# A decoder block on one core: scores of both attention maps on half the rows each, whole q and k loads, and four smaller moves

## The chip, the cores and the metric

The kernel runs on one core of one Trainium2 chip. The metric is the device time of one execution in microseconds, lower is better. The kernel is compared with a changed version of itself on the same inputs. The engines are named as in the profile: PE is TensorE's matmul, PEld its weight load, DVE is VectorE, ACT is ScalarE, POOL is GpSimd and SP is SyncE, which here issues most of the transfers.

## What is computed

One layer of a decoder with sequence 1024, width 1024 and float32 data. A norm of x feeds one input projection and sigmoid gates; three mixers work on the projection; the gated sum goes through an output projection; then comes a gated feed-forward part (FFN) with a causal convolution, and a final norm. The part that matters here is the third mixer: causal differential attention with four heads, each with two maps of 64 dimensions and one value of 128, and a position bias shared by both maps.

```python
def diff_attn_mixer(zq, zk, zv, lam_vecs, subln_g, rel_bias, layer_idx):
    ...
    s = jnp.einsum('bqhcd,bkhcd->bhcqk', qi, k) * scale      # c: the two maps
    s = s + bias.transpose(2, 0, 1)[None, :, None]
    s = jnp.where((rel >= 0)[None, None, None], s, -1e30)
    p = jax.nn.softmax(s, axis=-1)
    a = p[:, :, 0] - lam * p[:, :, 1]
    ...
    return rmsnorm(out, subln_g, eps=1e-5) * (1.0 - lam_init)

def reference(x, ...):
    h = rmsnorm(x, attn_norm_g); z = h @ w_in
    gates = sigmoid(h @ w_gate + b_gate)
    merged = g_a * (y_a @ proj_a) + g_b * (y_b @ proj_b) + g_c * (y_c @ proj_c)
    x = x + merged @ w_out
    x = x + conv_ffn(rmsnorm(x, ffn_norm_g), w_up, conv_w, conv_b, w_down)
    return rmsnorm(x, final_norm_g)
```

## The kernel before

Activations are kept transposed: 128 features on the rows, sequence positions on the columns, 512 columns to a PSUM bank. A float32 operand is split into a rounded high part and a low part (`split`, lines 96 and 97: a cast on ACT, a subtraction on DVE), and each product is three matmuls, high by high, high by low and low by high (`mm3`, line 191, with the list `PASSES`). The big products are done by a seven-product Strassen scheme, `strassen_pair` for pairs of output blocks and `strassen_full` for the output projection and the last FFN product. `strassen_pair` calls a hook `mid` four times, so that other work can be put between its products.

The order of the work is: norm and first mixers to 130 us; the q, k and pooling projections to 196 us; twelve gate pairs to 437 us, whose results go to DRAM (`g_d`); attention to 592 us, with the merge of the first two mixers (`merge_ab`, the "filler") between; the merge of the third (`merge_c`) to about 655 us; the output projection to about 725 us; the FFN to 1157 us; and its last product to the end. The instructions of an engine run in the order in which a scheduler set them when the kernel was built; a wait on one therefore holds back those behind it.

Attention works on tiles of 128 queries, `tiles` (head, i); a tile has (i + 1) x 128 keys, in one or two chunks of at most 512. `scores(t, c)` handles one map c of tile t: for each chunk two matmuls on 128 rows, with the stationary operand `qs` that holds the high part of q on rows 0 to 63 and its low part on 64 to 127, and the moving operands `kh` and `kl`, which hold the high (low) part of k on both halves of the rows (lines 759 and 760). DVE adds the bias tile T and takes the running minimum (line 762), ACT takes the exponential (line 768). `combine` subtracts the maps on DVE, `transpose` turns the tile on PE (tag "at"), `attend` multiplies it with the values V (tag "ms"). The PSUM banks are: three for scores ("sc"), two "at", one "ms", two "mm" for the merge and the norm of the heads.

`load_head` brings a head's operands from DRAM. Each map's `qs`, `kh` and `kl` are filled by two transfers of 64 rows each (line 716), 12 for a head; then come T from the bias table `fsc` and V, gathered from `v_d` in pieces of 128 columns. `rel_bias` makes the bias table after the first q and k pair: three matmuls with 33 rows and 4 columns (line 390), a copy on ACT, a store to `frow`, and four broadcasts from `frow` to `fsc`, all issued by SP.

Tiles come from two pools, `w4` of 13 tiles (weights, and other short-lived ones) and `a4` of 34. The output projection is `strassen_full` with four weight blocks; its passes p run in the order 0, 1, 2, 3, 5, 4, and loads are issued four items ahead (`loads`; `wfull` is line 843, `wh` line 835), in SP's order.

After the output projection `rms_mid` computes the FFN norm's factor for each half through `rms4a` and `rsqrt`: a square root on ACT, a reciprocal and one Newton step on DVE. `done1` prepares the operands T1 to T4 of the FFN's first products; they are made while the first FFN pair runs.

Of the kernel before, what the change touches and what calls it, by code (L numbers as in the profile page):

```python
# [11 lines left out]
F32 = mybir.dt.float32  # L12
I32 = mybir.dt.int32
F32R = mybir.dt.float32r
AF = mybir.ActivationFunctionType
# [3 lines left out]
P = 128  # L19
# [3 lines left out]
NH = 512  # L23
DFF = 2816
FT = DFF // P
NHEAD = 4
# [21 lines left out]
def trunk_kernel(  # L48
# [19 lines left out]
    nc = tc.nc  # L68
# [14 lines left out]
    def a4(shape=None, dt=F32, n="a"):  # L83
        return ap_.tile(shape or [P, S], dt, tag="a", name=nm(n))

    def w4(shape=None, dt=F32, n="w"):
        return wp.tile(shape or [P, S], dt, tag="w", name=nm(n))
# [4 lines left out]
    def tiny(n, tag, bufs=4):  # L92
        return sm.tile([P, n], F32, tag=tag, name=nm(tag), bufs=bufs)
# [57 lines left out]

        rms4b(rms4a(sq, pool), hs, pool)

    def rms4a(sq, pool):
        ps = pool()
        ss_cols(ps, sq, 4, 1, 0)
        t = tiny(4, "ssum")
        nc.vector.tensor_scalar(out=t, in0=ps[:, :4], scalar1=1.0 / D, scalar2=1e-6, op0=ALU.mult, op1=ALU.add)
        return rsqrt(t, 4)

    def rms4b(r, hs, pool):
        bcast_rows(r, 4, RB[:, hs], pool)
# [220 lines left out]
    def rel_bias():  # L383

        for c0 in range(0, NREL, NH):
            n = min(NH, NREL - c0)
            oh, fb = c2("oh"), c2("fb")
            nc.sync.dma_start(out=oh[:33, :n], in_=oneh[:, c0:c0 + n])
            pf = pm1()
            nc.tensor.matmul(pf[:NHEAD, :n], lhsT=rb, rhs=oh[:33, :n], start=True, stop=True)  # L390
            nc.scalar.mul(fb[:NHEAD, :n], pf[:NHEAD, :n], -1.0)
            nc.sync.dma_start(out=frow[:, c0:c0 + n], in_=fb[:NHEAD, :n])
        for hd in range(NHEAD):
            nc.sync.dma_start(out=fsc[hd], in_=frow[hd:hd + 1, :].broadcast_to([P, NREL]))

# [96 lines left out]


    qk_d = dram.tile([8, 2, P, S], F32, name="qk_d")
    v_d = dram.tile([8, P, NH], F32, name="v_d")
    y_d = dram.tile([4, P, S], F32, name="y_d")
    g_d = dram.tile([24, P, S], F32, name="g_d")
    x1_d = dram.tile([KT, P, S], F32, name="x1_d")
# [3 lines left out]
    def values():  # L502
# [32 lines left out]
        def store(o, banks, c, r, i):  # L535

            for b in range(2):
                TT(out=o[b], in0=banks[b], in1=c[b], op=ALU.add)
                for t in range(2):
                    sl = o[b][:, t * 256:(t + 1) * 256]  # L540
                    nc.scalar.mul(sl, sl, R8[:, 4 * i + 2 * b + t:4 * i + 2 * b + t + 1])
                tt = 4 * i + 2 * b
                nc.sync.dma_start(out=v_d[tt:tt + 2, :, r * 256:(r + 1) * 256].rearrange("t p c -> p t c"),
                                  in_=o[b].rearrange("p (t c) -> p t c", t=2))

        def wide(n):
            t = w4([P, 2, NH], n=n)
# [123 lines left out]
    for z in zb:  # L671
        times_r(z, nc.vector)

    rel_bias()


    def store_qk(i, Fs, eng=None):
        for n_, F in enumerate(Fs):
# [27 lines left out]

    def load_head(hd):

        H = heads[hd] = dict(qkl=[])
        for c in range(2):  # L710
            q, kh, kl = (a4(dt=F32R, n=n) for n in ("qs", "kh", "kl"))
            r = slice(64 * c, 64 * c + 64)
            for dst, src in ((q[0:64], qk_d[hd, 0, r]), (q[64:128], qk_d[hd, 1, r]),
                             (kh[0:64], qk_d[4 + hd, 0, r]), (kh[64:128], qk_d[4 + hd, 0, r]),
                             (kl[0:64], qk_d[4 + hd, 1, r]), (kl[64:128], qk_d[4 + hd, 1, r])):
                nc.sync.dma_start(out=dst.bitcast(F32), in_=src)
            H["qkl"].append((q, kh, kl))
            if c == 0:
                H["T"] = a4(n="T")
                base = fsc[hd]  # L720
                skew = bass.AP(tensor=base.tensor, offset=base.offset + P - 1, ap=[[NREL - 1, P], [1, S]])
                nc.sync.dma_start(out=H["T"], in_=skew)
            yield
        H["V"] = a4([P, 8, P], n="V")
        nc.sync.dma_start(out=H["V"], in_=v_d[:, :, hd * P:(hd + 1) * P].rearrange("t p c -> p t c"))
        yield
        H["s0"], H["ss"] = tiny(8, "s0", 2), tiny(8, "so", 2)
        H["O"] = a4([P, 8, P], n="O")
# [7 lines left out]
    st, AH = {}, {}  # L736
    score_bank = [pm1]

    def scores(t, c):

        if t >= len(tiles):
            return
        hd, i = tiles[t]
        H = heads[hd]
        W = (i + 1) * P
        if c == 0:
            if W <= NH:
                b = a4([P, 2, NH], n="sc")
                st[t] = dict(pr=[b[:, 0, :], b[:, 1, :]], s=[])
            else:  # L750
                st[t] = dict(pr=[a4(n="sc"), a4(n="sc")], s=[])
        q, kh, kl = H["qkl"][c]
        sc_ = st[t]["pr"][c]
        mx = tiny(2, "mx")
        chunks = [(0, min(NH, W))] + ([(NH, W - NH)] if W > NH else [])
        for n_, (c0, n) in enumerate(chunks):
            ps = score_bank[0]()
            qs = q[:, i * P:(i + 1) * P]
            nc.tensor.matmul(ps[:, :n], lhsT=qs, rhs=kh[:, c0:c0 + n], start=True, stop=False)  # L759
            nc.tensor.matmul(ps[:, :n], lhsT=qs, rhs=kl[:, c0:c0 + n], start=False, stop=True)  # L760
            o = (7 - i) * P + c0
            nc.vector.tensor_tensor_reduce(  # L762
                out=sc_[:, c0:c0 + n], in0=ps[:, :n], in1=H["T"][:, o:o + n], scale=1.0,
                scalar=mx[:, 0:1] if n_ else 3.0e38,
                op0=ALU.add, op1=ALU.min, accum_out=mx[:, n_:n_ + 1])
        nm_ = mx[:, n_:n_ + 1]
        sum_ = H["s0"][:, i:i + 1] if c == 0 else tiny(1, "s1")
        nc.scalar.activation(out=sc_[:, :W], in_=sc_[:, :W], func=AF.Exp, bias=nm_, scale=-1.0, accum_out=sum_)
        st[t]["s"].append(sum_)

    for n_ in range(12):
        Fs = strassen_pair(w_gate[n_], h, pb1)
        for k, F in enumerate(Fs):
            m = 2 * n_ + k
            times_r(F)
            nc.scalar.activation(out=F, in_=F, func=AF.Sigmoid, bias=col(C_BG + m), scale=1.0)
            nc.sync.dma_start(out=g_d[m], in_=F)
# [31 lines left out]
    def strassen_full(src, w, nsl, x_d, out, done, tail=None, LL=4):  # L809
# [29 lines left out]

        def wfull(p, j):  # L840
            if (p, j) not in halves:
                t = w4(n="fr")
                nc.sync.dma_start(out=t, in_=w[j])
                halves[p, j] = t
            return halves[p, j]
# [154 lines left out]

    ngain = const.tile([P, KT], F32, name="ngain")
    nc.scalar.mul(ngain, cs[:, C_GF:C_GF + KT], -1.0)
    tprep = [], []

    def op_g(src, g, n):

# [6 lines left out]
    def done1(d, j):  # L1013
# [45 lines left out]
            tprep[0].extend((t1, t2, t3))  # L1059
            return [store, operand, square]  # L1060
        if (d // 4, j) == (1, 0):
            tprep[1].append(t4)
            return [store, operand, square]
        return [store, square, operand]

# [8 lines left out]
            return p2.tile([P, NH], F32, tag=tag, name=nm(tag), bufs=bufs)  # L1074
        return f

    score_bank[0], pat, pms, pmm = pt2("sc", 3), pt2("at", 2), pt2("ms", 1), pt2("mm", 2)

    def combine(t):

# [126 lines left out]

    wo = strassen_full(lambda k: mg[k], w_out, 4, xT, lambda d, j: x1[d][:, half(j)], done1)
    LL = 4
    mc = merge_c([pmm, pmm, *score_bank * 3, pat, pat])  # L1210
    lates = []
    for t in range(len(tiles) + 3):
        hd, i = tiles[min(t, 31)]
# [71 lines left out]
            nc.scalar.copy(F0[k][:, half(j)], ps[k])  # L1285

    def rms_mid():
        for j in (1, 0):
            rs[j] = rms4a(stat[j], pb3)
            yield  # L1290
            rms4b(rs[j], half(j), pb3)
            yield
        stat.clear()
# [243 lines left out]
```

## Time and profile before

| what | value |
|---|---|
| time, median of 3 runs | 1388.32 us (1386.16 to 1389.51) |
| the profiled execution, its own time | 1389.13 us |
| its span, first to last instruction | 1387.4 us |
| mean granted TensorE clock | 0.991 |
| PE / PEld busy | 1344.9 us (97%) / 1120.5 us (81%) |
| DVE / ACT / POOL busy | 964.5 (70%) / 652.4 (47%) / 495.9 us (36%) |
| data moved by DMA | 204.65 MB, mean 148 GB/s |

A row of the timeline has start, duration, engine, line, operation, output and inputs, their shapes, how many instructions it joins, and, in brackets, how long the engine was idle before it and what ended that. The end of a matmul is modelled, so the cost of one is read from start to start. A busy share is an average over a stretch; an engine can be busy and still not be what the next one waits for.

### The profile page before, as it was taken

The numbers are of one execution on the slowest core, as the hardware profiler recorded it, in microseconds if no ns is written. First come the engines' busy times: TensorE is split into PE (matmuls) and PEld (weight loads), VectorE is DVE, ScalarE is ACT, GpSimd is POOL, SyncE is SP. The second block draws the span as 40 slices with busy tenths as digits, with TensorE's granted clock in tenths as the row PEclk, the third lists the DMA queues.
The fourth block names the chain that finished last, engine by engine and source line by source line (L and its number), as shares of the span: only waits on it lengthen the run. The fifth ranks groups of instructions, "written<-read, shape, count | busy, mean of one in ns | idle before, by whom it ended". The sixth has DMA issues, their size and how long they took to land.

```text
span 1387.4 us, 17666 instructions
## 1 busy us (share of the span) xinstructions
PE 1344.9 (97%) x6454; PEld 1120.5 (81%) x6454; DVE 964.5 (70%) x1487; ACT 652.4 (47%) x1109; POOL 495.9 (36%) x327
## 2 busy tenths in 40 slices
PE   9999999999999989999999999999999999999997
PEld 7997778888887778877777888888888887878786
DVE  7985774445444879958769576666777669985853
ACT  8633343344433666723667343433343435455461
POOL 0022334455553000022221665666656640102014
PEclk9999999999999999999999999999999999999998
DMA  7023363333239898588795222212222248845853
GB/s 261 10 78 109 108 222 134 121 121 104 101 115 272 252 242 209 151 233 193 201 221 131 83 77 91 79 74 91 91 77 91 75 151 305 274 126 150 226 128 122
DMA packets 78831, 204.65 MB, mean 148 GB/s; under 512 B 8270, under 2 KB 17614, under 8 KB 78744
## 3 DMA queue, kind: packets, MB, share of 16 engines
q1 hardware_dynamic: 67224, 180.44, 39.4%
q0 software_dynamic: 11520, 23.07, 9.7%
q8 instruction: 51, 0.84, 0.2%
q14 instruction: 36, 0.29, 0.1%
HBM read 143.70 MB, written 47.46 MB: 138 GB/s over the span
## 4 chain that ended last, share of the span: by engine, by line
PE 67%; DVE 13%; DMA 10%; issue 6%; ACT 3%; POOL 1%; SPq 1%; DVEq 0%; POOLq 0%; ACTq 0%
PE b L191 59%; PE mm L191 2%; DMA fr<-in_w_down 2%; DMA pr<-in_w_proj 1%; DVE ft L97 1%; PE ms L1112 1%; DVE fw L97 1%; DMA qs<-qk_d 1%; POOL ga L104 1%; DMA fr<-in_w_out 1%; DVE sc L762 1%; DMA x<-in_xT 1%; DMA yr<-y_d 1%; PE sc L759 1%; ACT fw L96 1%
## 5 line engine op out<-in xcount | busy, mean ns | idle before, releaser
L191 PE MATMUL b<-ft,fw 128*128 128x512 f32 (+1 forms) x1308 | 293.0, 384 | 9.8 <-ACT x L912 3.4
L191 PEld LDWEIGHTS b<-ft,fw 128*128 128x128 f32 x1308 | 239.9, 189 | 60.3 <-DVE fw L97 4.0
L354 POOL TENSOR_TENSOR F<-F,RB 128x1024 f32<-128x1024 f32 x68 | 185.5, 2730 | 111.3 <-DVE F L262 110.2
L262 DVE TENSOR_TENSOR F<-b,c 128x512 f32<-128x512 f32 x152 | 100.9, 683 | 130.5 <-ACT c L281 58.3
L191 PE MATMUL b<-hb,Ah 128*128 128x512 f32 x608 | 190.2, 392 | 0.0
L191 PE MATMUL b<-T,Sh 128*128 128x512 f32 x504 | 155.8, 390 | 1.9 <-ACT c L272 1.9
L234 POOL TENSOR_TENSOR s<-r 128x512 f32<-128x512 f32 x36 | 54.4, 1512 | 224.3 <-DMA r<-in_w_up 84.2
L191 PEld LDWEIGHTS b<-hb,Ah 128*128 128x128 f32 x608 | 114.5, 189 | 24.0 <-issue 0.5
L191 PE MATMUL b<-hb,Al 128*128 128x512 f32 x304 | 119.5, 393 | 2.5 <-DVE Al L97 2.5
L97 DVE TENSOR_TENSOR Al<-r,Ah 128x1024 fp32r<-128x1024 f32 x38 | 56.1, 1476 | 94.0 <-issue 77.9
L97 DVE TENSOR_TENSOR Sl<-s,Sh 128x1024 fp32r<-128x1024 f32 x76 | 107.0, 1408 | 13.9 <-ACT Sh L96 8.5
L96 ACT CAST Sh<-s 128x1024 fp32r<-128x1024 f32 x76 | 80.0, 1052 | 75.6 <-PE b L191 43.2
L191 PEld LDWEIGHTS b<-T,Sh 128*128 128x128 f32 x504 | 94.6, 188 | 21.8 <-ACT c L272 2.4
L191 PE MATMUL b<-T,Sl 128*128 128x512 f32 x252 | 98.1, 389 | 0.0
L191 PE MATMUL b<-hb,Sh 128*128 128x512 f32 x304 | 94.1, 391 | 2.9 <-DVE F L262 2.9
L96 ACT CAST Ah<-r 128x1024 fp32r<-128x1024 f32 x38 | 39.9, 1049 | 110.9 <-PE b L191 104.0
L96 ACT CAST fw<-fr 128x512 fp32r<-128x512 f32 x90 | 54.8, 622 | 62.4 <-DVE fw L97 25.0
L191 PE MATMUL b<-Th,Sh 128*128 128x512 f32 x204 | 79.1, 391 | 0.8 <-ACT c L267 0.8
L191 PE MATMUL b<-Tl,Sh 128*128 128x512 f32 x204 | 79.5, 390 | 0.0
L191 PE MATMUL b<-Th,Sl 128*128 128x512 f32 x204 | 79.4, 389 | 0.0
L191 PEld LDWEIGHTS b<-hb,Sh 128*128 128x128 f32 x304 | 56.8, 188 | 16.6 <-DVE F L262 4.2
L191 PEld LDWEIGHTS b<-hb,Al 128*128 128x128 f32 x304 | 57.4, 189 | 15.3 <-DVE Al L97 2.9
(284 smaller groups left out, 2838.9 us busy)
## 6 DMA issues: line engine op xcount, KB each, us to landing
fr<-in_w_down SPq DMA_DIRECT2D x47, 512.0 KB, 3.8
r<-in_w_up SPq DMA_DIRECT2D x42, 512.0 KB, 3.5
r<-in_w_gate SPq DMA_DIRECT2D x24, 512.0 KB, 3.6
g_d<-F SPq DMA_DIRECT2D x24, 512.0 KB, 2.8
act_d<-cv SPq DMA_DIRECT2D x22, 512.0 KB, 2.8
act<-act_d SPq DMA_DIRECT2D x22, 512.0 KB, 7.8
fr<-in_w_out SPq DMA_DIRECT2D x18, 512.0 KB, 6.1
ssb<-sq POOLq DMA_DIRECT2D x24, 256.0 KB, 4.1
```

The costliest lines, as they stand in the source:

```text
L96: nc.scalar.copy(hi, src)
L97: (eng or nc.vector).tensor_tensor(out=lo, in0=src, in1=hi.bitcast(F32), op=ALU.subtract)
L104: nc.gpsimd.dma_start(out=dst, in_=src, accum_op=ALU.add)
L191: last_mm[0] = nc.tensor.matmul(ps, lhsT=w[a], rhs=x[b], start=first and i == 0, stop=last and i == 2, skip_group_check=more)
L234: eng.tensor_tensor(out=s1[:, :NH], in0=a21, in1=a22, op=ALU.add)
L262: nc.vector.tensor_tensor(out=o, in0=ps, in1=c, op=ALU.add)
L354: (eng or nc.gpsimd).tensor_tensor(out=F, in0=F, in1=RB, op=ALU.mult)
L759: nc.tensor.matmul(ps[:, :n], lhsT=qs, rhs=kh[:, c0:c0 + n], start=True, stop=False)
L762: nc.vector.tensor_tensor_reduce(out=sc_[:, c0:c0 + n], in0=ps[:, :n], in1=H["T"][:, o:o + n], scale=1.0, scalar=mx[:, 0:1] if n_ else 3.0e38,
L1112: nc.tensor.matmul(po[:, :P], lhsT=AH[t][:, kb, :], rhs=H["V"][:, kb, :], start=kb == 0, stop=kb == i)
```

## The change

- `scores(t, n_)` now handles one chunk n_ of both maps. q and k are held whole: one tile with the high parts of both maps (map 0 on rows 0 to 63, map 1 on 64 to 127) and one with the low parts. Each chunk is three passes, each with one matmul of 64 rows for each map, into two banks. The score banks go from three to four, the merge banks from two to one.
- `load_head` makes four transfers of 128 rows for q and k instead of twelve of 64. `v_d` is laid out by head, with two stores for each half instead of one, and V is read in whole rows.
- `rel_bias` becomes a generator that the hooks of the gate pairs from the third on advance, and its first store is issued by ACT.
- The four whole weight blocks of pass 3 of the output projection come from `a4` instead of `w4`.
- The FFN norm's root is computed on DVE alone (a bit-level guess and three Newton steps), and the four T4 operands are made at the first hook of the next FFN pair.

```diff
-    def rms4a(sq, pool):
+    def rms4a(sq, pool, act=True):
...
-        return rsqrt(t, 4)
+        return rsqrt(t, 4, act)
...
-            nc.sync.dma_start(out=frow[:, c0:c0 + n], in_=fb[:NHEAD, :n])
+            nc.scalar.dma_start(out=frow[:, c0:c0 + n], in_=fb[:NHEAD, :n])
+            yield
...
-    v_d = dram.tile([8, P, NH], F32, name="v_d")
+    v_d = dram.tile([NHEAD, P, 8, P], F32, name="v_d")
...
-                nc.sync.dma_start(out=v_d[tt:tt + 2, :, r * 256:(r + 1) * 256].rearrange("t p c -> p t c"),
-                                  in_=o[b].rearrange("p (t c) -> p t c", t=2))
+                for k in range(2):
+                    nc.sync.dma_start(out=v_d[2 * r + k, :, tt:tt + 2, :],
+                                      in_=o[b].rearrange("p (t k c) -> p k t c", t=2, k=2)[:, k])
...
-    rel_bias()
...
-        H = heads[hd] = dict(qkl=[])
+        H = heads[hd] = dict(q=[], k=[])
         for c in range(2):
-            q, kh, kl = (a4(dt=F32R, n=n) for n in ("qs", "kh", "kl"))
-            r = slice(64 * c, 64 * c + 64)
-            for dst, src in ((q[0:64], qk_d[hd, 0, r]), (q[64:128], qk_d[hd, 1, r]),
-                             (kh[0:64], qk_d[4 + hd, 0, r]), (kh[64:128], qk_d[4 + hd, 0, r]),
-                             (kl[0:64], qk_d[4 + hd, 1, r]), (kl[64:128], qk_d[4 + hd, 1, r])):
-                nc.sync.dma_start(out=dst.bitcast(F32), in_=src)
-            H["qkl"].append((q, kh, kl))
+            q, k = a4(dt=F32R, n="q"), a4(dt=F32R, n="k")
+            nc.sync.dma_start(out=q.bitcast(F32), in_=qk_d[hd, c])
+            nc.sync.dma_start(out=k.bitcast(F32), in_=qk_d[4 + hd, c])
+            H["q"].append(q)
+            H["k"].append(k)
...
-        nc.sync.dma_start(out=H["V"], in_=v_d[:, :, hd * P:(hd + 1) * P].rearrange("t p c -> p t c"))
+        nc.sync.dma_start(out=H["V"], in_=v_d[hd])
...
-    def scores(t, c):
+    def scores(t, n_):
...
+        c0 = n_ * NH
+        n = min(NH, W - c0)
+        if n <= 0:
+            return
...
-        for n_, (c0, n) in enumerate(chunks):
-            ps = score_bank[0]()
-            qs = q[:, i * P:(i + 1) * P]
-            nc.tensor.matmul(ps[:, :n], lhsT=qs, rhs=kh[:, c0:c0 + n], start=True, stop=False)
-            nc.tensor.matmul(ps[:, :n], lhsT=qs, rhs=kl[:, c0:c0 + n], start=False, stop=True)
+        ps = [score_bank[0]() for _ in range(2)]
+        for k, (a, b) in enumerate(PASSES):
+            for c in range(2):
+                r = slice(64 * c, 64 * c + 64)
+                nc.tensor.matmul(ps[c][:, :n], lhsT=H["q"][a][r, i * P:(i + 1) * P], rhs=H["k"][b][r, c0:c0 + n],
+                                 start=k == 0, stop=k == 2)
...
+    bias = rel_bias()
     for n_ in range(12):
-        Fs = strassen_pair(w_gate[n_], h, pb1)
+        Fs = strassen_pair(w_gate[n_], h, pb1, lambda: next(bias, None) if n_ >= 2 else None)
...
-                t = w4(n="fr")
+                t = a4(n="fr") if p == 3 and nsl <= 4 else w4(n="fr")
...
-            tprep[1].append(t4)
+            t4s.append(t4)
...
-    score_bank[0], pat, pms, pmm = pt2("sc", 3), pt2("at", 2), pt2("ms", 1), pt2("mm", 2)
+    score_bank[0], pat, pms, pmm = pt2("sc", 4), pt2("at", 2), pt2("ms", 1), pt2("mm", 1)
...
-    mc = merge_c([pmm, pmm, *score_bank * 3, pat, pat])
+    mc = merge_c([pmm, *score_bank * 4, pat, pat])
...
+        for f in t4s:
+            f()
         for j in (1, 0):
-            rs[j] = rms4a(stat[j], pb3)
+            rs[j] = rms4a(stat[j], pb3, False)
```

## Rows read from the trace of the kernel before

**Rows 1.** Busy time by stretch of attention: us, PE, PEld, DVE, ACT, POOL, PEclk, DMA share, GB/s.
```profile
446.00:461.00 15.00, 12.67 (x45) 8.69 (x44) 13.44 (x28) 9.48 (x14) 3.93 (x2) 0.89 0.67 262
461.00:494.00 33.00, 27.43 (x176) 23.66 (x175) 23.34 (x76) 18.42 (x58) 1.92 (x2) 0.99 1.05 273
494.00:520.00 26.00, 25.96 (x162) 22.92 (x161) 22.84 (x76) 17.45 (x52) 0.86 (x1) 0.95 0.93 229
520.00:555.00 35.00, 34.43 (x220) 30.23 (x219) 31.73 (x102) 24.41 (x74) 1.72 (x2) 1.00 0.87 208
555.00:592.00 37.00, 36.06 (x233) 31.24 (x231) 35.19 (x125) 27.95 (x89) 1.72 (x2) 1.00 0.58 164
```

**Rows 2.** PE's timeline where it stood still, in attention and after it.
```profile
449.36 0.50 PE L759 MATMUL sc<-kh,qs 128*128 128x512 f32 x1 [1.54 <-DVE mx L762]
...
484.75 0.47 PE L760 MATMUL sc<-kl,qs 128*128 128x512 f32 x1 [1.59 <-DMA kl<-qk_d]
...
493.37 2.07 PE L191 MATMUL mm<-yv,ph 128*128 128x512 f32 x4 [3.32 <-ACT ph L96]
495.24 0.41 PE L759 MATMUL sc<-kh,qs 128*128 128x256 f32 x1
...
688.38 3.88 PE L191 MATMUL b<-ft,fw 128*128 128x512 f32 x10 [3.36 <-ACT x L912]
...
760.14 0.73 PE L191 MATMUL b<-T,Sh 128*128 128x512 f32 x2 [1.95 <-ACT c L272]
```

**Rows 3.** The chain of work that ended last: start, us, what.
```profile
480.30 12.38 DMA pr<-in_w_proj
...
677.68 6.11 DMA fr<-in_w_out
```

**Rows 4.** PE's timeline, score matmuls of each width.
```profile
557.47 0.48 PE L759 MATMUL sc<-kh,qs 128*128 128x512 f32 x1
557.78 0.39 PE L760 MATMUL sc<-kl,qs 128*128 128x512 f32 x1
558.01 0.39 PE L759 MATMUL sc<-kh,qs 128*128 128x512 f32 x1
...
561.76 0.34 PE L759 MATMUL sc<-kh,qs 128*128 128x384 f32 x1
561.94 0.34 PE L760 MATMUL sc<-kl,qs 128*128 128x384 f32 x1
...
583.54 0.28 PE L760 MATMUL sc<-kl,qs 128*128 128x256 f32 x1
583.66 0.23 PE L759 MATMUL sc<-kh,qs 128*128 128x128 f32 x1
...
583.83 0.62 PE L1103 MATMUL at<-ident,sc 128*128 128x128 f32 x4
```

**Rows 5.** Lines 759 and 390: counts, ns (min/median/max), first and last start, forms.
```profile
L759 PEld LDWEIGHTS sc<-kh,qs x94: 186/188/331, 446.5 to 585.3; 128*128 128x128 f32 x94
L759 PE MATMUL sc<-kh,qs x94: 220/389/522, 446.8 to 585.3; 128*128 128x512 f32 x46, 128*128 128x384 f32 x16, 128*128 128x256 f32 x16, 128*128 128x128 f32 x16
...
L390 PE MATMUL m<-oh,rb x6: 268/589/589, 130.6 to 140.6; 33*4 33x512 f32 x4, 33*4 33x127 f32 x2
```

**Rows 6.** PE's timeline around the first matmul of the position bias.
```profile
130.32 0.39 PE L191 MATMUL b<-hb,Al 128*128 128x512 f32 x1
130.64 1.02 PE L390 MATMUL m<-oh,rb 33*4 33x512 f32 x2
131.59 0.73 PE L191 MATMUL b<-hb,Sh 128*128 128x512 f32 x2
```

**Rows 7.** SP's timeline of issues in the output projection.
```profile
677.68 10.46 SPq L835 DMA_DIRECT2D fr<-in_w_out  x4
```

**Rows 8.** Busy time by stretch, columns as in rows 1, behind the output projection's stop.
```profile
685.00:695.00 10.00, 6.64 (x24) 5.41 (x24) 6.55 (x11) 8.60 (x18) 6.25 (x8) 0.83 0.90 213
745.00:755.00 10.00, 10.00 (x49) 8.37 (x49) 10.00 (x17) 5.35 (x9) 1.72 (x2) 1.00 0.43 102
```

**Rows 9.** ACT's timeline at the FFN norm's root.
```profile
757.17 1.28 ACT L123 ACT_TABLE_LOAD   x1
```

More of the change, by code (lines that the diff above doesn't have):

```diff
@@ L745, in scores @@
         W = (i + 1) * P
-        if c == 0:
+        c0 = n_ * NH
+        n = min(NH, W - c0)
+        if n <= 0:
+            return
+        if n_ == 0:
+            st[t] = dict(s=[], mx=[tiny(2, "mx", 6) for _ in range(2)])
             if W <= NH:
                 b = a4([P, 2, NH], n="sc")
-                st[t] = dict(pr=[b[:, 0, :], b[:, 1, :]], s=[])
+                st[t]["pr"] = [b[:, 0, :], b[:, 1, :]]
             else:
-                st[t] = dict(pr=[a4(n="sc"), a4(n="sc")], s=[])
@@ L752, in scores @@
[L752 to L755, printed above, removed]
-        for n_, (c0, n) in enumerate(chunks):
-            ps = score_bank[0]()
-            qs = q[:, i * P:(i + 1) * P]
-            nc.tensor.matmul(ps[:, :n], lhsT=qs, rhs=kh[:, c0:c0 + n], start=True, stop=False)
-            nc.tensor.matmul(ps[:, :n], lhsT=qs, rhs=kl[:, c0:c0 + n], start=False, stop=True)
-            o = (7 - i) * P + c0
+                st[t]["pr"] = [a4(n="sc"), a4(n="sc")]
@@ L762, in scores @@
+        ps = [score_bank[0]() for _ in range(2)]
[4 more added lines that the diff above has]
+                                 start=k == 0, stop=k == 2)
+        o = (7 - i) * P + c0
+        for c in range(2):
+            sc_, mx = st[t]["pr"][c], st[t]["mx"][c]
             nc.vector.tensor_tensor_reduce(
-                out=sc_[:, c0:c0 + n], in0=ps[:, :n], in1=H["T"][:, o:o + n], scale=1.0,
+                out=sc_[:, c0:c0 + n], in0=ps[c][:, :n], in1=H["T"][:, o:o + n], scale=1.0,
@@ L764, in scores @@
                 scalar=mx[:, 0:1] if n_ else 3.0e38,
                 op0=ALU.add, op1=ALU.min, accum_out=mx[:, n_:n_ + 1])
[L766 to L769, printed above, removed]
+            if c0 + n == W:
+                sum_ = H["s0"][:, i:i + 1] if c == 0 else tiny(1, "s1")
+                nc.scalar.activation(out=sc_[:, :W], in_=sc_[:, :W], func=AF.Exp, bias=mx[:, n_:n_ + 1], scale=-1.0,
+                                     accum_out=sum_)
+                st[t]["s"].append(sum_)
@@ L1002, in trunk_kernel @@
     nc.scalar.mul(ngain, cs[:, C_GF:C_GF + KT], -1.0)
-    tprep = [], []
+    tprep, t4s = ([], []), []
     def op_g(src, g, n):
```

## The prediction

> **What bounds the kernel now.** I read the page's busy shares first: TensorE (PE) is busy 97% of the span, so the question for each edit is where PE waits and what PE itself must do. The table by stretch [rows 1] then gives the stage that the change rewrites, the attention stage from 446 to 592 us. The reader is to see three things in it. PE stands still for 2.33 + 5.57 + 0.04 + 0.57 + 0.94 = 9.45 us of 146, nearly all before 494. VectorE (DVE) is almost as full: 13.44 + 23.34 + 22.84 + 31.73 + 35.19 = 126.5 us. And the DMA engines are saturated from 461 to 494 (share 1.05) and near it to 555. So early attention is bound by loads, late attention by PE with DVE close behind. The granted clock is below 1 in the first and third stretch: 15 x 0.11 + 33 x 0.01 + 26 x 0.05 = 3.3 us more. PE's timeline [rows 2] names the stops: 1.54 us for a score bank that DVE had not read yet, 1.59 us for a kl load, and 3.32 us for ACT's copy of pr, whose load took 12.38 us to land by the chain of waits [rows 3]. After that stop the next four matmuls start 0.47 us apart (493.37 to 495.24) instead of 0.23: the lower of the two clock levels, 1.2 instead of 2.4 GHz.
>
> **The scores' matmuls.** Before, a chunk of a map is two matmuls on 128 rows; both maps make four. After, it is three passes for each map on 64 rows, six matmuls, and a pair (map 0 on rows 0 to 63, map 1 on rows 64 to 127) may share the array. Start to start, a matmul costs 0.23 us at 512 columns (557.78 to 558.01), 0.18 at 384, 0.12 at 256, and 0.17 for two at 128, 0.085 each [rows 4]. By width there are 46 + 2 of 512 and 16 each of 384, 256 and 128 over the two maps [rows 5], so one pass of one map is 24 x 0.23 + 8 x 0.18 + 8 x 0.12 + 8 x 0.085 = 8.6 us. Four passes are 34.4 us now. If pairs overlap fully, three remain: -8.6 us. If not at all, six: +17.2 us. No row of before shows two matmuls side by side; these are the two ends. I take the end of full overlap, less 0.8 us because a 128-column pair must load two sets of weights (8 chunks x 3 passes x about 0.035 us): **-7.8 us**. My reason is that the halves read disjoint rows of their operands and write two banks.
>
> **Going in and out of 64-row work.** The trace has one nearby case: the position bias, a matmul with 33 rows and 4 columns amid full-size ones [rows 6]. The preceding matmul starts at 130.32, so the next was due at 130.55; after the bias the second full-size one starts at 131.93 (131.59 + 0.73 - 0.39). That is 1.38 us, of which the two bias passes are 2 x 0.43 (1.02 less the 0.589 of one, [rows 5]) and one matmul 0.23: some 0.29 us go to getting in and out. The changed scores make 48 groups (32 first chunks, 16 second ones), or 13.9 us at most; at least nothing. Today the scores stand in 59 separate stretches on PE's timeline, from 446.8 to 585.3 us [rows 5]; 37 follow fp32 work and pay about 0.08 us for that (557.47 to 557.78 is 0.31 instead of 0.23, [rows 4]): 3.0 us that the new price contains. Some groups will stand together; with 40 entries it is 40 x 0.29 - 3.0 = **+8.6 us** (ends: -3 and +10.9). So the new score code is worth about +0.8 us by itself, a tie, not a gain.
>
> A rule of the Trainium skill speaks against this edit: TensorEngine Tiling (Array Packing), section Key Properties, says that changing the tiling mode (not only the tile) drains TensorE. The 0.29 us agrees with it. TensorE: Matmul & The Clock Gate, Part 3, has four 32-row tiles run 3.07 times as fast as one after the other; as an estimate from that figure, two tiles at the same efficiency run 1.53 times as fast, six matmuls cost as much as 3.9, and the sum below would be some 8 us later. No row of before shows two tiles at once.
>
> **Whole q and k loads.** A head now takes 12 transfers of 256 KB for q and k, 3 MB; after, four of 512 KB, 2 MB, and the values arrive as 4 KB rows instead of 512-byte pieces. That takes 4 MB out of a stage that moves 15 x 262 + 33 x 273 + 26 x 229 + 35 x 208 + 37 x 164 = 32 MB [rows 1], and eight issues for each head off SP's queue, where the gate and projection loads stand behind them. The stops it can remove: 1.54 + 1.59 + 3.32 us and the slow clock after them, 3.3 us: 9.75 us at most, nothing at least (another load may be as late). I take **-6 us**, not all, since DVE is 90% busy from 446 to 461 and 88% from 494 to 520 and is next late. The price on the other side: the values are stored in 16 transfers instead of 8; eight more issues of some 0.4 us on SP lie in a stretch where PE computes, 0 to +1 us; I take 0.
>
> **Weights in the wide pool.** In the output projection SP issues four loads between 677.68 and 688.14, each as a buffer comes free [rows 7]; the first takes 6.11 us to land [rows 3], ACT's casts of it stand ahead of the bank copy L912, and PE waits 3.36 us for that [rows 2] and then runs at a granted clock of 0.83 over ten us, 1.7 us [rows 8]. With four of pass 3's tiles elsewhere, these loads can go out up to four buffers earlier. At most -5.1 us; at worst the wide pool (34 tiles, with sums, residual and operands in it) is full too, and SP, which issues in order, stops there: 0 to +3. I take **-4 us**: DVE is only 6.6 of 10 busy behind the stop, so an earlier PE is not held at once.
>
> **FFN norm's root.** ACT loads a table (1.28 us) for the square root just ahead of the copy L272 for which PE waits 1.95 us [rows 2, 9]. The load goes; the root becomes ten small DVE steps instead of four, twice, in a stretch where DVE has hardly a gap (10.00 of 10 us from 745 to 755, [rows 8]), and four T4 operands (two DVE steps each) move behind the split of the weights, shortly before PE needs them. Ends -2.3 and +3; I take **-1 us**.
>
> **Bias among the gates; one merge bank.** The three excursions of the bias move from one PE-bound stage to another: the same 3 x 0.29 us there as here, its broadcasts lie beside matmuls, and the store is queued on ACT behind its own copy; SP's wait for that store holds back gate weights and gate stores, with POOL and buffers in between: -0.5 to +2, taken as **+0.5 us**. The merge bank goes from two to one: its next matmul group waits for DVE's product of the last, 0.69 us plus DVE's lag; PE has scores and values to do between, so 0 to +3, taken as **+1 us**.
>
> **Sum.** -7.8 + 8.6 - 6 - 4 - 1 + 0.5 + 1 = -8.7 us. The profiled execution took 1389.13 us (span 1387.4 and 1.7 around it), 0.8 above the median of 1388.32 us. 1389.13 - 8.7 - 0.8 = 1379.6: I say **1380 us**.
>
> **Rivals.** *Overlap only in part* (chance 0.2): the pairs run side by side, but as slowly as today's four matmuls, so the 7.8 us are lost while the switches stay. 1380 + 8 = **1388 us**. For it: two weight loads for each pair, 188 ns each in the records [rows 5]. Against it: today's four loads hide behind the matmuls, or 0.23 us could not stand. *No overlap* (0.15), the slow side: PE runs six matmuls one after the other on half the rows. PE's work in the stage rises by 17.2 instead of falling by 7.8: 1380 + 25 = **1405 us**. It decides from the point where a pair takes more than 4/3 of a single matmul plus what the loads give back. For it: no row shows any overlap, and late attention has PE busy 36.06 of 37 us, so nothing would hide it. *Relief goes elsewhere* (0.12): fewer bytes let loads land earlier, but DVE, 126.5 us of work and its order unchanged, or one merge bank, holds PE, and the wide pool is full; -6 and -4 become about +2 in all: **1392 us**. *Free switches* (0.08): getting in and out costs no more than today's 0.08: **1371 us**. That the bias or the root alone moves the end is too small to be a case.
>
> **How the numbers follow.** The forecast has 0.45, with 1374 to 1386 as its own range. From 1372 to 1396 all but the no-overlap case and half of the free switches lie inside, about 0.8. About 0.2% (2.8 us) is what a measurement of this kernel can tell from no change. Below 1385.5: most of the forecast, the free switches, a little of the partial overlap, 0.53. Between 1385.5 and 1391.1: most of the partial overlap and edges, 0.20. Above: no overlap, relief elsewhere, tails, 0.27.
>
> **What would show it.** Score matmuls of the two maps starting within a few ns to some tens of ns of each other, a 512-column pair each 0.23 us (a pair each 0.45 us: no overlap). Some 0.1 us lost at each entry and exit. From 446 to 592, PE idle down from 9.45 to some 4 us and the stage about 5 us shorter. No stop of 3.36 us in the output projection, no table load in the FFN norm. I am wrong if PE's busy time in attention grows, if SP stops on the wide pool, or if T4 holds PE after the root.

## The result and the profile after

The changed kernel takes **1407.26 us** (median of four, 1404.61 to 1408.70) where the kernel before takes 1387.24 beside it: a ratio of 1.0149 (1.0121 to 1.0176), 20 us slower. The forecast was 1380, with a range that ended at 1396. The profiled execution took 1408.7 us (span 1407.0).

The page's first part and its slices show what kind of loss this is (busy us, share, instructions):

```profile
span 1407.0 us, 17820 instructions
...
PE 1360.1 (97%) x6550; PEld 1118.5 (79%) x6550; DVE 975.9 (69%) x1499; ACT 650.7 (46%) x1106; POOL 494.3 (35%) x327
...
DMA packets 75887, 200.44 MB, mean 142 GB/s; under 512 B 7887, under 2 KB 15183, under 8 KB 75801
```

PE is busy 15 us longer than before (1344.9), with 96 more matmuls; the bytes fell by 4.2 MB (from 204.65), as the whole loads should do. Of the 19.6 us that the span grew, 15.2 are work of PE and 4.4 are stops: PE got more to do. By stage, the profiled execution reaches the last gate (the start of its sigmoid on ACT) 3.7 us later, takes 11.0 us longer from there to the last value matmul, and 5.8 us longer in the last FFN product, which no edit touches. There the granted clock is 0.91 in two stretches of 20 us; the product takes 246.1 us here and 238 to 242 in every other run, those with the same scores too, so nothing ties these 5.8 us to the new scores. The table by stretch of attention answers to [rows 1], with the same columns:

```profile
450.00:465.00 15.00, 12.25 (x75) 8.80 (x75) 13.62 (x31) 7.69 (x13) 4.13 (x2) 1.00 0.38 131
465.00:498.00 33.00, 32.53 (x201) 24.29 (x199) 26.57 (x86) 21.93 (x67) 1.92 (x2) 1.00 0.94 325
498.00:526.00 28.00, 26.85 (x172) 20.75 (x173) 21.96 (x75) 16.02 (x55) 0.86 (x1) 1.00 0.48 153
526.00:565.00 39.00, 36.89 (x230) 28.24 (x229) 29.48 (x97) 22.78 (x72) 1.72 (x2) 1.00 0.50 136
565.00:606.00 41.00, 37.97 (x238) 29.78 (x237) 31.97 (x110) 25.00 (x74) 1.72 (x2) 1.00 0.42 118
```

Three things differ. Where the loads stopped PE, from 465 to 498, it is now busy 32.53 of 33 us, and the granted clock is 1.00 throughout: the relief came. But behind 526, where PE was full, it now stands still for 2.11 and 3.03 us; over the whole stage that makes 9.51 us, as much as the 9.45 before, where the forecast had some 4. And its busy time from 450 to 606 is 146.5 us, against 136.6 from 446 to 592: 10 us of new work. From the last gate to the last value matmul the stage takes 177.7 us instead of 166.7.

The reason is on PE's timeline, which answers to [rows 4] (start, us, engine, line, operation):

```profile
463.73 0.97 PE L760 MATMUL sc<-k,q 64*128 64x512 f32 x6
464.62 1.65 PE L191 MATMUL mm<-yv,ph 128*128 128x512 f32 x6
466.21 0.96 PE L760 MATMUL sc<-k,q 64*128 64x128 f32 x12
...
471.21 0.96 PE L760 MATMUL sc<-k,q 64*128 64x512 f32 x3
472.10 1.83 PE L1118 MATMUL ms<-V,ah 128*128 128x128 f32 x14
473.86 0.96 PE L760 MATMUL sc<-k,q 64*128 64x512 f32 x3
474.75 1.65 PE L191 MATMUL mm<-yv,ph 128*128 128x512 f32 x6
```

The first row is what the change means to do: six matmuls of 512 columns, three for each map, in 464.62 - 463.73 = 0.89 us. The starts of one pair mostly lie 3 to 10 ns apart. But the fourth row holds **three** such matmuls, one map's, and takes 472.10 - 471.21 = 0.89 us as well; the other map's three follow 1.76 us later, behind fourteen value matmuls, for another 0.89. The kernel's scheduler, which sets the order of PE's work, has parted the maps. Of 141 pairs of this line in attention, 90 start within 30 ns of each other; 20 of the stage's stretches hold three matmuls.

The rows also show the neighbours paying. Six projection matmuls between two stretches of scores take 466.21 - 464.62 = 1.59 us; at the usual 0.23 each they would take 1.38. PE's weight loads say where some of it goes (same columns; the bracket is idle time ahead):

```profile
562.13 0.54 PEld L760 LDWEIGHTS sc<-k,q 64*128 64x128 f32 x6 [0.36 <-issue]
563.03 0.53 PEld L1109 LDWEIGHTS at<-ident,sc 128*128 128x128 f32 x5 [0.36 <-issue]
...
566.77 0.30 PEld L1118 LDWEIGHTS ms<-V,ah 128*128 128x128 f32 x2 [0.36 <-issue]
```

In these rows the first load behind a change of row count begins 0.36 us after the load before it has ended, and the profile shows no other engine that it waited for. Of the stage's 96 changes of row count, 63 show such a gap above 0.15 us; of 593 full-row loads behind another full-row load, 8 do.

The median spacings over all stretches: a 64-row matmul that follows a projection starts 0.326 us after it (0.227 before the change), one that follows a transpose 0.203 (0.029). The stretch's second step, at 512 columns, comes 0.335 to 0.339 us after its first; before the change it was 0.227 behind a projection and 0.314 behind transposes and values. The next full-row matmul starts 0.324 after the last of 512 columns (0.234), and, for projections, its own second one after 0.335 (0.235).

Elsewhere the forecast's signs are there. In the output projection, the stop of [rows 2] at 688 is gone:

```profile
658.04 66.95 PE L191 MATMUL b<-ft,fw 128*128 128x512 f32 x294 [1.27 <-DVE gc L1210]
...
727.26 0.50 PE L191 MATMUL b<-ft,fw 128*128 128x512 f32 x1 [2.27 <-ACT ft L96]
...
776.18 0.73 PE L191 MATMUL b<-hb,Sh 128*128 128x512 f32 x2 [2.09 <-DVE F L262]
```

The last row is the FFN norm: no table is loaded, but PE waits 2.09 us for a bank that DVE's addition L262 frees, where it had waited 1.95 for ACT. And in late attention a stop is new, ahead of the transposes that the merge needs:

```profile
590.08 0.66 PE L1146 MATMUL mm<-ident,O 128*128 128x128 f32 x4 [0.78 <-DVE ga L1185]
...
596.98 0.66 PE L1146 MATMUL mm<-ident,O 128*128 128x128 f32 x4 [0.78 <-DVE gb L1185]
```

### The profile page after: what moved, and what is told of

It is laid out like the page before. It is cut to its first block, busy times and chain, and to the rows that moved or that the text cites. A ratio compares the mean times of both kernels' runs of the same rounds, so it can differ in the third digit from the quotient of the medians.

```text
span 1407.0 us, 17820 instructions
## 1 busy us (share of the span) xinstructions
PE 1360.1 (97%) x6550; PEld 1118.5 (79%) x6550; DVE 975.9 (69%) x1499; ACT 650.7 (46%) x1106; POOL 494.3 (35%) x327
## 5 line engine op out<-in xcount | busy, mean ns | idle before, releaser
L191 PE MATMUL b<-ft,fw 128*128 128x512 f32 (+1 forms) x1308 | 296.1, 387 | 9.6 <-DVE fw L97 4.4
L262 DVE TENSOR_TENSOR F<-b,c 128x512 f32<-128x512 f32 x152 | 100.5, 682 | 115.2 <-ACT c L281 60.3
L97 DVE TENSOR_TENSOR Sl<-s,Sh 128x1024 fp32r<-128x1024 f32 x76 | 111.1, 1462 | 27.3 <-ACT Sh L96 14.6
L191 PEld LDWEIGHTS b<-T,Sh 128*128 128x128 f32 x504 | 94.6, 188 | 19.6
```

The costliest lines, as they stand in the source:

```text
L97: (eng or nc.vector).tensor_tensor(out=lo, in0=src, in1=hi.bitcast(F32), op=ALU.subtract)
L191: last_mm[0] = nc.tensor.matmul(ps, lhsT=w[a], rhs=x[b], start=first and i == 0, stop=last and i == 2, skip_group_check=more)
L262: nc.vector.tensor_tensor(out=o, in0=ps, in1=c, op=ALU.add)
```

## The experiments

Two theories stood at the start. A: the score stage as it is now written carries the loss, by parted maps (A1) and by entries and exits that cost more than counted (A2). B: one of the four small parts carries it.

**The score code alone**, with its loads, its banks and the values' layout; bias, wide pool and root as before.

```
+        for k, (a, b) in enumerate(PASSES):
+            for c in range(2):
+                r = slice(64 * c, 64 * c + 64)
+                nc.tensor.matmul(ps[c][:, :n], lhsT=H["q"][a][r, ...], rhs=H["k"][b][r, c0:c0 + n], ...)
...
+    score_bank[0], pat, pms, pmm = pt2("sc", 4), pt2("at", 2), pt2("ms", 1), pt2("mm", 1)
```

> The kernel before with the scores on 64 rows, the whole q and k loads, the banks 4 and 1 and the values' layout; bias, weight pool and root as before. Theory A (the score stage carries the loss: getting in and out of 64-row work costs about 0.4 us for each of 48 stretches, and maps that the schedule parts do not overlap): +8 to +15 us against before, attention about 11 us longer. Theory B (the loss is spread over the moved parts, and the scores are the tie that was forecast): within -6 to +3 us.

Measured: 1402.38 us beside 1385.71, ratio 1.0114 (1.0076 to 1.0151), +16. The stage from the last gate to the last value matmul is 177.6 us, as in the changed kernel.

**All but the score code**: the changed kernel with the scores, loads and banks of before.

```
-        H = heads[hd] = dict(q=[], k=[])
+        H = heads[hd] = dict(qkl=[])
...
-    def scores(t, n_):
+    def scores(t, c):
```

> The changed kernel with the scores, q and k loads and banks of before; bias among the gates, values' layout, wide pool and DVE root kept. Theory A: -4 to +6 us against before (the profile of the changed kernel puts the bias's move at about +3, the wide pool at -3, the root at +1 to +2). Theory B: +12 us or more.

Measured: 1386.35, ratio 1.0006 (0.9989 to 1.0023). The four small parts together are worth nothing that can be seen. B falls; the loss is in the score code, with its loads and banks.

**Each score matmul on 64 rows, nothing else.** This leaves out the products with the low part of q. Columns, order and loads are those of before.

```
-            qs = q[:, i * P:(i + 1) * P]
-            nc.tensor.matmul(ps[:, :n], lhsT=qs, rhs=kh[:, c0:c0 + n], start=True, stop=False)
+            qs = q[0:64, i * P:(i + 1) * P]
+            nc.tensor.matmul(ps[:, :n], lhsT=qs, rhs=kh[0:64, c0:c0 + n], start=True, stop=False)
```

> The kernel before with one thing changed: each score matmul uses rows 0 to 63 of its operands alone, the same matmuls, columns, stretches, loads and banks. It leaves out the products with the low part of q and is for its time alone. Theory A (entering and leaving 64-row work has a price of about 0.4 us, 59 stretches): +12 to +22 us. Rival (the price is in the parted maps and the banks, not in the row count): within -2 to +3 us.

Measured: 1399.27 beside 1385.71, ratio 1.0102 (1.0066 to 1.0138): +14 us for a kernel that does no more matmuls, and stands still less. The rows, to be read beside [rows 4]:

```profile
560.96 0.49 PE L759 MATMUL sc<-kh,qs 64*128 64x512 f32 x1
561.30 0.39 PE L760 MATMUL sc<-kl,qs 64*128 64x512 f32 x1
561.62 1.43 PE L191 MATMUL mm<-yv,ph 128*128 128x512 f32 x5
...
564.20 0.39 PE L760 MATMUL sc<-kl,qs 64*128 64x512 f32 x1
564.43 0.39 PE L759 MATMUL sc<-kh,qs 64*128 64x512 f32 x1
564.66 0.39 PE L760 MATMUL sc<-kl,qs 64*128 64x512 f32 x1
```

Within a stretch a 64-row matmul costs 0.23 us like any other (564.20 to 564.43); the first and the last of a stretch cost 0.34 and 0.32. Start-to-start times of PE's matmuls in the stage, gaps over 0.6 us left out, sum to 15.1 us more than before, with the same 60 stretches; before also lost 3.3 us there to the slow clock of [rows 1], which this run does not (1.00 in all five stretches). So a stretch costs (15.1 + 3.3) / 60 = 0.31 us more than it did. Compared stretch by stretch, the median is 0.39 us behind a projection and 0.34 behind transposes and values. A2 holds.

**Whole loads alone.** The kernel before with four whole transfers for a head; the operands then aren't stacked as its scores want them, so it computes other scores.

```
+            q, k = a4(dt=F32R, n="q"), a4(dt=F32R, n="k")
+            nc.sync.dma_start(out=q.bitcast(F32), in_=qk_d[hd, c])
+            nc.sync.dma_start(out=k.bitcast(F32), in_=qk_d[4 + hd, c])
```

> The kernel before with four whole loads of q and k for a head in place of twelve; its score matmuls are as before in number, rows and columns, but read operands that are not stacked for them, so it computes other scores: it is for its time alone. Forecast's step (4 MB less in attention): -6 us (0 to -10). Rival (DVE holds the stage): -2 to +1 us.

Measured: 1376.67 beside 1385.71, ratio 0.9931 (0.9912 to 0.9951), -9.5 us. Its table by stretch, columns as in [rows 1]:

```profile
446.00:461.00 15.00, 13.73 (x68) 11.18 (x69) 14.08 (x28) 8.25 (x13) 5.19 (x2) 1.00 0.42 166
461.00:494.00 33.00, 30.12 (x187) 25.52 (x186) 27.34 (x92) 21.94 (x70) 1.92 (x2) 1.00 0.97 316
```

PE is busy 43.85 us of the first 48 instead of 40.10, at full clock. This is the largest gain of any part. The changed kernel has it too, under its losses: the stops for kl and pr of [rows 2] are gone from its timeline.

**The maps in turn.** The changed kernel with the order of the six matmuls written out: each is queued behind the one before it.

```
+        prev = None
         for k, (a, b) in enumerate(PASSES):
             for c in range(2):
+                with (tc.issue_after(prev.ins) if prev else nullcontext()):
+                    prev = nc.tensor.matmul(...)
```

> The changed kernel with one addition: the six matmuls of a score group are queued each behind the one before it, so that the maps take turns and neither stands alone. Theory A1 (parted maps are a large part: 51 of 141 pairs of matmuls did not start together): 6 to 12 us faster than the changed kernel, +8 to +14 us against before. Theory A2 (getting in and out carries nearly all): within 4 us of the changed kernel, +16 to +21 us against before. It can also be worse, if the first matmul of map 1 now holds back map 0 for its bank.

Measured: 1396.08 beside 1386.57, ratio 1.0069 (1.0044 to 1.0094), +9.5: 0.80 points, 11 us (some 5 either way), better than the changed kernel. 125 of 141 pairs start together, and whole tiles now stand in one stretch; but not all:

```profile
470.52 0.50 PE L762 MATMUL sc<-k,q 64*128 64x512 f32 x1
470.95 1.83 PE L1120 MATMUL ms<-V,ah 128*128 128x128 f32 x14
472.71 0.96 PE L762 MATMUL sc<-k,q 64*128 64x512 f32 x5
...
560.78 1.50 PE L762 MATMUL sc<-k,q 64*128 64x512 f32 x12
562.21 1.66 PE L191 MATMUL mm<-yv,ph 128*128 128x512 f32 x6
563.70 1.05 PE L1120 MATMUL ms<-V,ah 128*128 128x128 f32 x8
564.68 1.33 PE L762 MATMUL sc<-k,q 64*128 64x512 f32 x12
```

A1 holds for about half of the 20 us, and the overlap is real. But the maps are not all together: an order says what comes after what, and the scheduler still put other work between. In the built program 12 of the 48 groups have the first matmul of map 0 apart from the other five, as in the first row, 8 of them as a stretch of one. A group parted so takes four steps where a whole one takes three. By their widths the 12 extra steps are some 2.3 us, and 8 more stretches at 0.31 us are 2.5 us (both are estimates). So some 5 of the 9.5 us that are still lost may be parting too.

**The bias alone, the wide pool alone, the root alone.**

```
+            nc.scalar.dma_start(out=frow[:, c0:c0 + n], in_=fb[:NHEAD, :n])
+            yield
...
+                t = a4(n="fr") if p == 3 and nsl <= 4 else w4(n="fr")
...
+            rs[j] = rms4a(stat[j], pb3, False)
```

> The kernel before with the position bias among the gates and its store on ACT, nothing else. Forecast's step: +0.5 us (-0.5 to +2). By the changed kernel's profile (pooling ends 3 us earlier, gates take 6 us longer): +2 to +4 us.

> The kernel before with the four weight blocks of pass 3 of the output projection in the wide pool, nothing else. Forecast's step: -4 us (-5.1 to +3). By the changed kernel's profile (that stage 3 us shorter): -2 to -4 us.

> The kernel before with the FFN norm's root on DVE and the T4 operands at the first hook, nothing else. Forecast's step: -1 us (-2.3 to +3). By the changed kernel's profile (first FFN activation 1.6 us later than the stage before): 0 to +2 us.

Measured beside 1386.57: bias 1386.57 (0.9983 to 1.0018), wide pool 1386.60 (0.9981 to 1.0014), root 1388.50 (0.9986 to 1.0025). None can be told from no change. The wide pool's row reads as hoped, one run of 294 matmuls in place of 186 and 108:

```profile
643.60 66.94 PE L191 MATMUL b<-ft,fw 128*128 128x512 f32 x294 [0.35 <-DVE gc L1205]
711.78 0.50 PE L191 MATMUL b<-ft,fw 128*128 128x512 f32 x1 [1.24 <-ACT ft L96]
```

But the stop that it removes was not worth 3.36 us in other executions of the same code: ahead of the same 108 matmuls the bias run waited 1.10 us, the loads run 1.48, the 64-row run 0.72 and the root's run 2.83. Nor does the pool always remove it: the run with all but the score code has the wide pool, and waits 0.57 us there. The root's run shows a trade:

```profile
757.21 0.73 PE L191 MATMUL b<-T,Sh 128*128 128x512 f32 x2 [0.58 <-ACT c L272]
...
762.82 0.73 PE L191 MATMUL b<-hb,Sh 128*128 128x512 f32 x2 [2.60 <-DVE F L262]
```

The wait for ACT fell from 1.95 us to 0.58, and one of 2.60 for DVE is new: PE needs the bank that L262 frees, and on DVE the split of the weights and steps of the root stand ahead of it.

**The banks alone.** The kernel before with four banks for scores and one for the merge.

```
-    score_bank[0], pat, pms, pmm = pt2("sc", 3), pt2("at", 2), pt2("ms", 1), pt2("mm", 2)
+    score_bank[0], pat, pms, pmm = pt2("sc", 4), pt2("at", 2), pt2("ms", 1), pt2("mm", 1)
```

> Before with four banks for scores and one for the merge in place of three and two, nothing else. In the changed kernel PE waits 0.78 us for DVE's product (ga or gb) ahead of the merge's transposes five times, and never over 0.6 us there before. If the one merge bank makes these stops and nothing gives them back: +2 to +4 us, 1389 to 1391 beside 1387. If the fourth score bank pays for it (the stop of 1.54 us for a score bank goes): -1 to +1. My term was +1 with ends 0 and +3.

Measured: 1392.44 beside 1387.31, ratio 1.0038 (1.0020 to 1.0057), +5.2 us, a little over what either reading gave. The stops stand in its timeline as in the changed kernel's:

```profile
450.07 0.50 PE L759 MATMUL sc<-kh,qs 128*128 128x512 f32 x1 [2.58 <-DVE F L262]
...
508.78 1.95 PE L191 MATMUL mm<-yv,ph 128*128 128x512 f32 x6 [1.86 <-DVE yc L1009]
...
580.41 0.66 PE L1140 MATMUL mm<-ident,O 128*128 128x128 f32 x4 [0.79 <-DVE ga L1179]
...
586.84 0.66 PE L1140 MATMUL mm<-ident,O 128*128 128x128 f32 x4 [0.78 <-DVE gb L1179]
```

The last two rows' waits are DVE's product, 0.69 us, with PE's queue in order behind it; with a third of 0.61 they sum to 2.2 us. The second row is new too: the filler's projections wait for the one merge bank until DVE has read the heads' transposed values from it (L1009), 1.86 us here and 1.56 at 546. And the first row's stop, ahead of the scores, is 2.58 us where it was 1.54: the bank comes free only behind DVE's addition for the last gate, so the fourth score bank did not pay. Other waits fell, and the attention stage grew by 4.0 us in all, the merge behind it by 0.8.

**Six loads in place of twelve**, a try at the loads' gain for the scores of before: 3 MB and six buffers for a head as before, but each transfer fills 128 rows.

```
+            nc.sync.dma_start(out=q.bitcast(F32), in_=qk_d[hd, :, r])
+            for z, dst in enumerate((kh, kl)):
+                nc.sync.dma_start(out=dst.bitcast(F32), in_=qk_d[4 + hd, z:z + 1, r].broadcast_to([2, 64, S]))
```

> Before's scores on 128 rows and before's store; only the twelve half loads of q and k for a head become six loads that each fill all 128 rows (a load of kh or kl reads its 64 rows twice). The bytes stay at 3 MB a head and the six buffers stay; only the issues on SP halve and each transfer covers all rows. Whole loads on four buffers and 2 MB gave 9.5 us. If it was the bytes and the buffers: 1384 to 1388 us beside 1386 to 1387 of before, loads still landing late between 461 and 494, PE busy there about 27.5 of 33 us. If it was the issues and the half-filled transfers: 1376 to 1381 us, PE busy there above 29.5 of 33. Between 1381 and 1384 both have a share.

> The run above with the values stored so that a head's arrive in 4 KB rows, and pass 3's weights in the wide pool. If the values' 512-byte pieces held the loads back, another 1 to 4 us below the run above; the wide pool alone measured 1386.6 beside 1387.2, so 0 to -2 from it. If neither carries anything, within 1.5 us of the run above. PE's wait for the copy x in the output projection (1.1 to 3.4 us) is gone here and stays in the run above.

Measured: 1582.66 and 1587.48 beside 1387.07 (ratios 1.1419 and 1.1447). Neither case was near. SP's timeline in the first of the two (duration of an issue in the second column), and the stage's table by stretch:

```profile
443.84 10.51 SPq L715 DMA_DIRECT2D kh<-qk_d  x1
454.44 9.91 SPq L715 DMA_DIRECT2D kl<-qk_d  x1
464.44 4.08 SPq L724 DMA_DIRECT2D V<-v_d  x1
468.61 17.78 SPq L1152 DMA_DIRECT2D yr<-y_d  x1
```

```profile
440.00:480.00 40.00, 8.75 (x25) 6.38 (x25) 0.11 (x1) 0.00 (x0) 0.00 (x0) 0.60 0.22 73
480.00:560.00 80.00, 33.38 (x165) 26.18 (x166) 31.28 (x78) 21.59 (x51) 6.22 (x3) 0.71 0.37 127
```

The issues of kh and kl hold SP for some 10 us each, and everything behind them on SP's queue waits, while the DMA engines are 0.22 to 0.37 busy. The source of these transfers has an outer dimension of 2. From 454 to 464 us, with little else under way, 53 GB/s move at a DMA share of 0.13; at that rate 512 KB take 9.9 us.

**The same, with the operands stored as they are needed**, so that the six loads are plain.

```
+            for dst, src in ((q, qk_d[hd, c]), (kh, kk_d[hd, c, 0]), (kl, kk_d[hd, c, 1])):
+                nc.sync.dma_start(out=dst.bitcast(F32), in_=src)
```

> Before, with q, kh and kl stored as its scores need them: a map's high part above its low part, and each part of k twice. A head's loads are then six plain transfers of 128 whole rows (3 MB, six buffers as before) in place of twelve of 64 rows; the stores of a head become 12 of 64 rows in place of 4 of 128, 1 MB more, in the stretch before the gates. The run that read rows twice lost 195 us, with SP held some 10 us by single issues and the DMA engines 0.2 to 0.4 busy: if that came from the transfers' form (an outer dimension of 2), it is gone here and the time is 1376 to 1390. Within that: if half-filled transfers and issues made before's stops, 1376 to 1381; if the bytes and buffers did, 1384 to 1390 (the stores cost 0 to 3 more). If the loss stays (above 1450), it came from the six loads themselves and not from their form.

Measured: 1392.59 beside 1387.31, ratio 1.0036 (1.0018 to 1.0054), +5. The 195 us are gone, so they came from the transfers' form. The stage from the last gate to the last value matmul is 166.3 us, as before (166.7): half the issues and full transfers gave nothing that shows. The loss lies where the larger store stands: from the pooling's end (its last copy on ACT) to the last gate 248.2 us instead of 242.1. But the run does not settle what the whole loads' 9.5 us come from. The stores of the last head stand in attention, not ahead of the gates, and SP issues them from 464.71 to 480.45 us, ahead of the next head's loads:

```profile
472.49 7.96 SPq L692 DMA_DIRECT2D kk_d<-ql  x4
480.55 0.84 SPq L719 DMA_DIRECT2D qs<-qk_d  x1
```

These loads start 35 us behind the last gate, where in the kernel before they start 21 us behind it (at 459.18). So a gain from fewer issues may have been lost again to the stores. Whether bytes and buffers or the issues carry the 9.5 us is not shown. Of the versions that compute the layer, none is faster than the kernel before.

## Why the prediction was wrong

It named the right stage and the right currencies, but the score code, forecast as a tie with a gain from the loads on top, loses 16 us. Start-to-start times of PE's matmuls show its balance, from 10 us ahead of the last gate to the last value matmul. Each matmul counts until the next one starts, up to 0.6 us; what is beyond stands in the last line.

| us | whole loads alone | maps in turn | changed kernel |
|---|---|---|---|
| scores | 41.4 | 40.9 | 47.9 |
| projections and other products (302, 295, 296 matmuls) | 71.6 | 75.8 | 75.3 |
| values | 30.2 | 34.3 | 34.4 |
| transposes of the weights | 16.1 | 17.5 | 17.9 |
| transposes for the merge | 2.5 | 4.8 | 4.8 |
| gaps beyond 0.6 us | 4.7 | 10.3 | 7.8 |

All three have 2 MB of loads for a head. Only the first works on full rows, and with two merge banks.

- **The scores' matmuls, -7.8: right in price, wrong in an assumption that it never stated.** A pair costs 0.23 us, as taken (six in 0.89 us). The step counted every pair as meeting. The scheduler let 20 stretches of three stand alone, each as dear as six; keeping most of them together is worth 11 us, good to some 5 (1.0149 against 1.0069). The 0.8 us set aside for the weights of 128-column pairs had no row behind it; within a stretch such a pair takes 0.11 us, as one full-row matmul does there. The rival of no overlap gave 1405, close to the time measured, but its mechanism is false: nothing ran one after the other for want of room in the array.
- **Going in and out, +8.6: mis-sized, the term that fell furthest.** Priced at 0.29 us for 40 entries, less 3.0 us that today's switches were said to contain. Measured, a stretch costs 0.31 us **beyond** what it cost before (the 64-row run), and the changed kernel has 50 of them: 15 to 16 us, nearly twice the term. The table gives nearly the same: from the loads run to the maps-in-turn run, projections, values and transposes of the weights took 4.2 + 1.6 (seven matmuls fewer, at 0.23) + 4.1 + 1.4 = 11.3 us more, and the scores, which should have fallen by 7.8, fell by 0.5: 11.3 + 7.3 = 18.6 us. Of these 3.4 are a slow clock (0.89 over 15 us from 451, 0.95 over 35 us from 560) and some 2.3 the extra steps of the 12 parted groups; the other 12.9 over 44 stretches are 0.29 each. Two readings of [rows 6] were at fault. The bias passes were taken out at their own spacing, so the slower step from a stretch's first 64-row matmul to its second, 0.11 us behind a projection, is not in the 0.29. And the 3.0 us are not given back: behind transposes and values the first 64-row matmul comes 0.17 us later than before, not 0.09 as behind a projection, and such a stretch costs 0.34 us more in all, where 0.29 - 0.08 = 0.21 was taken.
- **Whole loads, -6: right, and too small**: -9.5 by themselves. The slow clock of [rows 1] went with the stops.
- **One merge bank, +1: too small**: +5.2 (2.8 to 7.9). The text had PE busy with other work during the wait; PE's queue is in order, and what stood behind the transposes waited with them. That the filler needs the same bank was not counted.
- **Weights in the wide pool, -4: wrong** (0.0, -2.6 to +1.9). The stop goes, or falls to 0.57 us; but 3.36 us was what one execution showed of a stop that others have at 0.2 to 2.8 us, and removing it by itself buys nothing that can be measured.
- **Root, -1, and bias, +0.5**: neither can be told from nothing. That T4 might hold PE behind the root was named; a stop behind the root is there, but PE waits in it for a bank that DVE frees late, not for T4.

Put together: forecast -8.7, parted maps +11, entries about +7 (15 to 16 instead of 8.6), bank +4, wide pool +4, loads -3.5, root and bias +1 give some +15 of the 20 us measured. What is left is not assigned to a row, and single edits need not add up: the 11 holds the entries of six stretches, and is itself good to 5 us. The values' layout was not tried by itself.

Two rules of the Trainium skill were weighed. The Trainium skill, TensorEngine Tiling (Array Packing), section Key Properties, has a change of tiling mode drain TensorE: the traces agree, in that time is lost in both directions, 0.34 to 0.39 us for a stretch. The Trainium skill, TensorE: Matmul & The Clock Gate, Part 3, has row tiles run concurrently; the estimate of 1.53 times for two tiles was too low here, where six matmuls took 0.89 us and three 0.89, twice as fast. Much of the loss came by the first rule, which spoke against this edit; the parted maps are the other large part.

## What to carry to other kernels

Packing two half-height matmuls side by side has to earn its entries and exits: here a chunk of 512 columns saved 0.23 us and a stretch cost 0.31, so only stretches of several chunks could pay. Price an entry and an exit where they stand, next to each neighbour, down to the second matmul on either side, and multiply by the stretches on the timeline. Write the order out, since a scheduler that does not know of pairs may part them, and look on the timeline whether the groups stayed whole. A stop seen in one execution is not a steady cost; look for it in a second trace before it goes into a sum. When a change trades banks or buffers to make room, try that trade by itself: here one bank fewer cost 5 us, five times what was set down for it.

## What the runs showed of the hardware

- Two 64-row matmuls on different halves start mostly 3 to 10 ns apart, and six of 512 columns take 0.89 us even where the built program has the three of one map ahead of the three of the other (the changed kernel's at 463.73). One map's three take just as long.
- A 64-row matmul alone costs no less than a 128-row one (0.23 us at 512 columns), but a change of row count costs PE time at both ends. Medians of the 64-row run against before, behind a projection: 0.09 us ahead of the first 64-row matmul, 0.11 ahead of its second, 0.09 ahead of the first full-row one and 0.10 ahead of its second; behind transposes and values 0.17, 0.02, 0.09 and 0.06 to 0.08. The weight loads beside it show the gap ("0.36 <-issue").
- Here two loads of 512 KB whose source has an outer dimension of 2 held SP for 10 us each, with 53 GB/s moved at a DMA share of 0.13; loads of the same bytes as plain rows were issued in 0.3 to 1.5 us. The Trainium skill, DMA: Bandwidth & Descriptors, section Rules for kernel authors, says that a small outermost dimension confines a transfer to as many engines; two of 16 engines are a share of 0.125, which agrees, and the run with plain rows bears it out.
